# First ada sums on TensorE, norms scaled on DVE, attention normed early and first in the output product, a square root in the convolution: the mixer of a fused two-block kernel

## The chip, the cores and the metric

One Trainium2 chip, one core of it. The metric is the device time of one execution in microseconds (us). Engines are named as in the profile: PE is TensorE's matrix multiplication, PEld its weight load, DVE VectorE, ACT ScalarE, POOL GpSimd, SP SyncE, whose queue issues nearly all DMAs. Before the change the median of 3 runs is 2957.59 us (2957.12 to 2958.0).

## The reference, cut to what matters

512 tokens of width 1024 run through a first block (a mixer of attention and a gated convolution, then a layer of 16384 experts) and a second one (two more layers with attention, a recurrence and feed-forward parts). The change touches the first block's mixer and the start of the expert layer:

```python
ada = silu(c) @ w_ada + b_ada                       # six vectors of 1024
shift1, scale1, gate1, shift2, scale2, gate2 = split(ada, 6)
h = rms_norm(x, norm1_g) * (1 + scale1) + shift1
proj = h @ w_in + b_in                              # q, k, v, then three gates of the convolution
attn = head_rms_norm(sliding_window_sink_attention(q, k, v, sinks), attn_out_g, 8)
conv = head_rms_norm(b_gate * conv3(c_gate * u), conv_out_g, 8)
x = x + gate1 * (concatenate([attn, conv]) @ w_out + b_out)
h2 = rms_norm(x, norm2_g) * (1 + scale2) + shift2
q = h2 @ w_query                                    # scores against two key tables, top 16 of each
x = x + gate2 * experts(h2, top 16 of the sums)
```

All is in float32. A product is made of three matmuls in a reduced format: each operand is split into a high and a low part, and high x high, low x high and high x low are summed.

## The kernel before, in words

The kernel is one Python class that writes out every instruction; a framework puts each engine's instructions in an order at compile time, sets the semaphores, and gives out buffers of a named ring (a tag with a number of buffers) as the instructions that first write them are placed. A block under `issue_after(ins)` puts what it traces on that instruction's engine behind it.

`mixer0` begins with the ada vectors. `ada1(k)` (L396) loads, for two columns of 128, four pieces of w_ada of 512 KB through the ring `raw` (4 buffers, shared with all weight loads), and `ada_acc` (L333) sums them on DVE, one row block of 128 at a time, eight for each vector; a matmul with ones (`ptc`, L359) then adds over the partitions. The four token tiles of x are normed by `rms_tokens` (L314): square with a sum on ACT, root on ACT, reciprocal on DVE, scaling on ACT for this first norm (L328) and on DVE for all others (L326). `to_fm` (L275) transposes the normed tokens on PE, applies scale and shift on ACT and DVE, and splits them. Four such column pairs run one after the other, with the first five weight chunks of w_in between.

The product with w_in has 18 chunks of 128 output columns; `consume(n, ps)` (L432) takes each. Chunks 0 to 4 are q and k, 5 is v, after which `sw_block` (L507) writes out the attention of four blocks of 128 tokens with two head groups each. Chunks 6 to 17 are four convolution groups of three chunks each; with the third chunk of a group (n = 8, 11, 14, 17) the group is convolved on DVE, squared on ACT, summed over 64 channels by a matmul with a block matrix (`ptms`, L478), put through Ln and Exp on ACT (L479, L480) and split into `mixh` and `mixl`. Beside it, four pieces per chunk of the remaining ada vectors (gate1, scale2, shift2) are loaded into the ring `mix` (8 buffers, shared with the mixh and mixl tiles) and summed on DVE; their closing matmuls (`ends`) run two chunks after. The PSUM ring `pst` (2 buffers, tag t) serves ptc, the attention's scores and transposes, ptms and the transposes of `to_fm`.

After the 18 chunks `sw_finish` (L559) norms the attention's output over heads and transposes it (`pto`, L572) into split tiles in the rings xh and xl. The output product (`gemm_tm`) runs in two halves of 512 columns, four token tiles of eight row blocks each; the order of the row blocks is three convolution groups, four attention tiles, the last convolution group, and w_out's rows are laid out to match. In the first half all four token tiles advance together, one row block at a time. `consume2` (L495) adds gate1 times the result to x. Then the second norm and `to_fm` give the input of the expert layer, `xs2`, with a copy of 128 tokens kept (`keep`, L309). `peer_route` multiplies by w_query in 16 chunks, and DVE finds the top 16 of each score row with MAX8 and its companions (`top16`, L593).

`to_fm` has a parameter `late`: with it, all columns of the first three token tiles are done first, and all columns of the last token tile after them. The ring `b4` (4 buffers of 1024 floats) holds normed tokens and the attention's scores S.

Of the kernel before, what the change touches and what calls it, by code (L numbers as in the profile page):

```python
# [10 lines left out]
F32 = mybir.dt.float32  # L11
# [56 lines left out]
def _layout(i):  # L68
# [25 lines left out]
    L["w_out"] = _kh(np.concatenate([i["w_out"][512:896], i["w_out"][:512], i["w_out"][896:]]), 2)  # L94
# [63 lines left out]
class _Kernel:  # L158
# [155 lines left out]
    def rms_tokens(self, x, pool, d=1024, fast=True):  # L314

        nc = self.nc
        xn = []
        for t in range(4):
            j = self.work.tile([128, d], F32, tag="sq", name="sq", bufs=1)
            ss = self.small.tile([128, 1], F32, tag="ss", name="ss", bufs=4)  # L320
            nc.scalar.activation(j, x[t], AF.Square, accum_out=ss)
            r = self.small.tile([128, 1], F32, tag="r", name="r", bufs=4)
            self.rstd(r, ss, 1.0 / d, self.eps6)
            o = pool.tile([128, d], F32, tag="b4", name="xn", bufs=4) if pool else x[t]
            if fast:
                nc.vector.tensor_scalar(o, x[t], r, None, ALU.mult)  # L326
            else:
                nc.scalar.activation(o, x[t], AF.Copy, scale=r)  # L328
            xn.append(o)
        return xn  # L330
# [34 lines left out]

    def ada_row(self, s, brow, out, pool, later=None):
        nc = self.nc
        nc.sync.dma_start(out, bass.AP(tensor=self.a["rows"].tensor,
                                       offset=self.a["rows"][_ROWS.index(brow)].offset,
                                       ap=[[0, 128], [1, 1024]]))  # L370
        for c0 in range(0, 1024, 512):
            yield from self.ada_acc(s, c0, 512, pool, None)

            def end(acc=self.acc, c=slice(c0, c0 + 512)):
                pt = (self.pst or self.psa).tile([128, 512], F32, tag="t" if self.pst else "a", name="ptr")
                nc.tensor.matmul(pt, self.ones, acc)
                nc.vector.tensor_tensor(out[:, c], pt, out[:, c], ALU.add)

            later.append(end) if later is not None else end()
            yield  # L380


    def mixer0(self):
# [3 lines left out]
        with tc.tile_pool(name="m0", bufs=1) as p:  # L387
# [11 lines left out]
            first, xt = ada1(0), []  # L399
# [5 lines left out]
            xn = self.rms_tokens(xt, p, fast=False)  # L405
# [22 lines left out]
            mixh, mixl, bo = [], [], []  # L428
            vt = p.tile([128, 4, 128], F32, name="vt")

            def consume(n, ps):
                b = self.col("b_in", n)  # L432
                if n == 12:
                    bo.append(self.brow(p, "b_out", "b4", 4))
# [24 lines left out]
                else:  # L459
                    j, g = divmod(n - 6, 3)  # L460
# [18 lines left out]
                    nc.scalar.activation(r, pt, AF.Ln, bias=self.eps6, scale=1.0 / 64)  # L479
                    nc.scalar.activation(r, r, AF.Exp, scale=-0.5)  # L480
# [7 lines left out]
            mx = list(zip(mixh, mixl))  # L488
            mix = mx[:3] + self.sw_finish(p, oall) + mx[3:]
# [15 lines left out]
            self.xs2 = self.to_fm(self.rms_tokens(x1, p), A2, ada["B2"], keep=self.h2)  # L505
# [52 lines left out]
    def sw_finish(self, p, oall):  # L558
# [3 lines left out]
        for n in range(4):  # L562
            sq = p.tile([128, 1024], F32, tag="b4", name="osq", bufs=4)
            nc.scalar.activation(sq[:, 0:512], oall[:, n, :], AF.Square)
            nc.vector.tensor_reduce(ss[:, n * 8:(n + 1) * 8], sq[:, 0:512].rearrange("p (h d) -> p h d", d=64), AX.X, ALU.add)
# [3 lines left out]
        for j in range(4):  # L569
# [6 lines left out]
            h = self.xpool.tile([128, 512], F32R, tag="xh", name="xh", bufs=8)  # L576
            l = self.xpool.tile([128, 512], F32R, tag="xl", name="xl", bufs=8)
# [25 lines left out]
    def peer_route(self, p, G, fill, step):  # L603
# [52 lines left out]
        self.gemm_fm(self.xs2, [a["w_query"][c] for c in range(16)], consume)  # L656
# [709 lines left out]
```

## Time and profile before

| | |
|---|---|
| median of 3 runs | 2957.59 us (2957.12 to 2958.0) |
| the profiled execution | 2946.67 us, its span 2944.9 us |
| mean granted TensorE clock of it | 0.983 |
| PE busy | 2816.2 us (96%) |
| PEld busy | 2382.1 us (81%) |
| DVE busy | 1963.8 us (67%) |
| ACT busy | 1132.1 us (38%) |
| POOL busy | 332.7 us (11%) |

The span goes from the first to the last instruction; what lies between it and the execution's time is start and end. Busy times are sums of modelled durations, and matmuls overlap: two that follow each other by 0.23 us show 0.39 us each. In the lines of the profile a group reads: line, engine, operation, output<-inputs with the buffer numbers left out, shapes, count, then busy time in us, mean ns of one, idle time of the engine just before and who ended it. In a timeline a line begins with start and duration in us; a bracket at its end gives idle time before it and what released it.

### The profile page before, as it was taken

To read this page: it belongs to the slowest core of one execution; us is meant where nothing else is said; L and a number is where in the kernel's file an instruction comes from. 1 tells how busy PE (TensorE), PEld (TensorE's weight loads), DVE (VectorE), ACT (ScalarE), POOL (GpSimd) and SP (SyncE) were. 2 spreads that over 40 slices of the span, in tenths; PEclk is the share of its full clock that TensorE was granted. 3 is DMA by queue.
4 is the path that set the end of the run, shared out by engine and by line. 5 is a ranking of instruction groups with operands and counts; after the bars stand their busy time and mean duration, and the time that the engine had idled before them with its cause. 6 is when DMAs were issued, how large, how long until landed. Compare 5 with 4: busy or idle time off the path is not lost.

```text
span 2944.9 us, 37577 instructions
## 1 busy us (share of the span) xinstructions
PE 2816.2 (96%) x14133; PEld 2382.1 (81%) x14133; DVE 1963.8 (67%) x3665; ACT 1132.1 (38%) x1672; POOL 332.7 (11%) x265
## 2 busy tenths in 40 slices
PE   6999959889999999999999999999999999999998
PEld 5777858788899999988787778888878887888887
DVE  8676999898778777886557666433474567634336
ACT  4454325566333333333346424222242233422223
POOL 0000023221334433440000000000000000000000
PEclk9999979899999999999999999999999999999999
DMA  8432368778999988899763103232321212323331
GB/s 294 149 105 86 101 199 301 284 295 315 361 320 323 323 313 307 312 325 308 229 188 119 57 29 115 89 118 94 100 91 63 86 58 65 115 86 112 102 95 51
DMA packets 182007, 521.34 MB, mean 177 GB/s; under 512 B 19776, under 2 KB 68544, under 8 KB 180288
## 3 DMA queue, kind: packets, MB, share of 16 engines
q1 hardware_dynamic: 144960, 384.70, 38.7%
q0 software_dynamic: 36864, 134.23, 12.8%
q8 instruction: 111, 1.82, 0.3%
q14 instruction: 72, 0.59, 0.1%
HBM read 478.48 MB, written 40.37 MB: 176 GB/s over the span
## 4 chain that ended last, share of the span: by engine, by line
PE 47%; DVE 2%; DMA 1%; ACT 0%; issue 0%; SPq 0%; DVEq 0%; ACTq 0%
PE psa L205 7%; PE psa L204 7%; PE psa L206 7%; PE psv L204 3%; PE psv L205 3%; PE psv L206 3%; PE psd L206 3%; PE psd L204 3%; PE psd L205 3%; PE pl L1274 1%; PE y L205 1%; PE y L206 1%; PE y L204 1%; PE pss L1013 1%; PE pt L289 1%; PE po L1030 1%
## 5 line engine op out<-in xcount | busy, mean ns | idle before, releaser
L186 ACT ACTIVATE wh<-raw 128x1024 fp32r<-128x1024 f32 x512 | 539.0, 1060 | 1199.3 <-PE psa L205 427.5
L189 DVE TENSOR_TENSOR wl<-raw,wh 128x1024 fp32r<-128x1024 f32 x510 | 620.3, 1222 | 338.4 <-ACT wh L186 323.9
L204 PE MATMUL psa<-xh,wh 128*128 128x512 f32 x1168 | 460.4, 397 | 4.3 <-ACT xh L300 2.8
L205 PE MATMUL psa<-xl,wh 128*128 128x512 f32 x1168 | 460.4, 395 | 1.9 <-DVE xl L307 1.9
L206 PE MATMUL psa<-xh,wl 128*128 128x512 f32 x1168 | 458.0, 393 | 0.5 <-DVE wl L189 0.5
L206 PE MATMUL psu<-xh,wl 128*128 128x384 f32 x1024 | 347.7, 340 | 22.3 <-DVE wl L189 22.3
L204 PE MATMUL psu<-xh,wh 128*128 128x384 f32 x1024 | 349.6, 341 | 16.0 <-ACT ga L798 11.6
L205 PE MATMUL psu<-xl,wh 128*128 128x384 f32 x1024 | 348.2, 340 | 0.0
L205 PE MATMUL y<-wl,wgh 128*128 128x512 f32 x768 | 299.6, 390 | 4.6 <-DVE wl L189 4.6
L206 PE MATMUL y<-wh,wgl 128*128 128x512 f32 x768 | 299.9, 391 | 0.0
L204 PE MATMUL y<-wh,wgh 128*128 128x512 f32 x768 | 298.9, 389 | 0.2 <-ACT wgh L186 0.2
L204 PEld LDWEIGHTS psa<-xh,wh 128*128 128x128 f32 x1168 | 220.8, 190 | 55.2 <-ACT xh L300 6.9
L205 PEld LDWEIGHTS psa<-xl,wh 128*128 128x128 f32 x1168 | 220.4, 189 | 48.1 <-DVE xl L307 3.6
L206 PEld LDWEIGHTS psa<-xh,wl 128*128 128x128 f32 x1168 | 220.4, 189 | 46.1 <-issue 1.0
L206 PEld LDWEIGHTS psu<-xh,wl 128*128 128x128 f32 x1024 | 194.8, 190 | 24.0 <-DVE wl L189 23.9
L204 PEld LDWEIGHTS psu<-xh,wh 128*128 128x128 f32 x1024 | 194.9, 190 | 23.1 <-ACT ga L798 13.9
L754 POOL DMA_INDIRECT row<-in_peer_u_rows,ui x128 | 162.2, 1267 | 426.1 <-DVE junk L761 242.0
L754 POOL DMA_INDIRECT row<-in_peer_v,vi x128 | 164.8, 1288 | 276.0 <-DVE y L770 256.4
L205 PEld LDWEIGHTS psu<-xl,wh 128*128 128x128 f32 x1024 | 194.8, 190 | 1.2 <-issue 0.5
L204 PE MATMUL psv<-wh,xh 128*128 128x512 f32 x464 | 185.4, 400 | 4.2 <-ACT xh L298 2.8
L205 PE MATMUL psv<-wl,xh 128*128 128x512 f32 x464 | 183.9, 396 | 0.0
L770 DVE SCALAR_TENSOR_TENSOR y<-row,au,y 128x1024 f32<-128x1024 f32 x127 | 162.8, 1282 | 30.8 <-DMA row<-in_peer_v,vi 30.2
(331 smaller groups left out, 4379.1 us busy)
## 6 DMA issues: line engine op xcount, KB each, us to landing
raw<-in_peer_u SPq DMA_DIRECT2D x128, 512.0 KB
raw<-in_peer_v SPq DMA_DIRECT2D x128, 512.0 KB
raw<-in_ffn_in SPq DMA_DIRECT2D x88, 512.0 KB
G<-gt SPq DMA_DIRECT2D x12, 2048.0 KB
g<-G SPq DMA_DIRECT2D x192, 128.0 KB
raw<-in_ffn_dn SPq DMA_DIRECT2D x44, 512.0 KB
rawa<-in_w_ada SPq DMA_DIRECT2D x64, 256.0 KB
AD<-ga SPq DMA_DIRECT2D x56, 192.0 KB
```

The source lines that it names most:

```text
L186: nc.scalar.activation(h, full, AF.Copy)
L189: (nc.gpsimd if pool else nc.vector).tensor_tensor(l, full, h.bitcast(F32), ALU.subtract)
L204: nc.tensor.matmul(out, A[0], B[0], start=first, stop=False)
L205: nc.tensor.matmul(out, A[0], B[1], start=False, stop=False)
L206: self.last_mm = nc.tensor.matmul(out, A[1], B[0], start=False, stop=last)
L289: nc.tensor.transpose(pt[:, (t - t0) * 128:(t - t0 + 1) * 128], xn[t][:, k * 128:(k + 1) * 128], self.ident)
L754: nc.gpsimd.indirect_dma_start(out=r, out_offset=None, in_=table, in_offset=bass.IndirectOffsetOnAxis(ap=idx[:, j:j + 1], axis=0))
L770: nc.vector.scalar_tensor_tensor(w, r, au[:, j:j + 1], w, ALU.mult, ALU.add)
L1013: nc.tensor.matmul(ps[:, :W], qr[h // 2][rb:rb + 64, q], kr[rb:rb + 64, :W], start=False, stop=True)
L1030: nc.tensor.matmul(po[:, q], v[j][:, h * 128:(h + 1) * 128], et[:, j * 128:(j + 1) * 128], start=j == 0, stop=j == i)
L1274: nc.tensor.matmul(pt[:P, o:o + 64], k[:, h, c * 128:c * 128 + P], qv[:, c, :, 1])
```

## The change

- The first pair of ada columns is summed by matmuls: `ada_pe` loads the same four pieces in the same order and multiplies each 128x128 block of w_ada by one column of silu(c), accumulating in PSUM over the eight row blocks; the other three pairs stay on DVE.
- All norms scale on DVE; a root of one column is computed at the start (`warm`).
- `sw_finish` is called in `consume` at n = 11, ahead of that chunk's convolution, with its squares in the ring `et` and its split results in `b4`; the attention tiles come first in the output product, then the four convolution groups, and w_out's rows are laid out in that order.
- The row b_out goes into the ring `sq` of the pool `work`.
- The convolution's norm takes a square root on ACT and a reciprocal on DVE (`rstd`) in place of Ln and Exp.
- The second norm's `to_fm` is called with `late=True`; the first four weight chunks of w_query are loaded ahead of the product, the third and fourth with their DVE instructions behind the last scaling of the norm.

```diff
-    L["w_out"] = _kh(np.concatenate([i["w_out"][512:896], i["w_out"][:512], i["w_out"][896:]]), 2)
+    L["w_out"] = _kh(i["w_out"], 2)
...
-            if fast:
-                nc.vector.tensor_scalar(o, x[t], r, None, ALU.mult)
-            else:
-                nc.scalar.activation(o, x[t], AF.Copy, scale=r)
+            self.last_norm = nc.vector.tensor_scalar(o, x[t], r, None, ALU.mult)
...
+    def ada_pe(self, s, bias, out, plus, lo):
+
+        nc = self.nc
+        pt = self.pst.tile([128, 512], F32, tag="t", name="pta")
+        ts = []
+        for k0 in range(0, 8, 4):
+            ts.append(self.wpool.tile([128, 4, 256], F32, tag="raw", name="rawa", bufs=4))
+            nc.sync.dma_start(ts[-1], self.a["w_ada"][s, k0:k0 + 4, :, lo:lo + 256].rearrange("k p n -> p k n"))
+            if k0 == 0:
+                yield
+        for j in range(2):
+            for k in range(8):
+                nc.tensor.matmul(pt[:, j:j + 1], ts[k // 4][:, k % 4, j * 128:(j + 1) * 128], self.sc[:, k:k + 1],
+                                 start=k == 0, stop=k == 7)
+        j0 = lo // 128
+        nc.vector.scalar_tensor_tensor(out[:, j0:j0 + 2], pt[:, 0:2], plus, self.col(bias, j0, 2), ALU.add, ALU.add)
+        yield
...
-            first, xt = ada1(0), []
+            warm = self.small.tile([128, 1], F32, name="warm", bufs=1)
+            nc.scalar.activation(warm, self.eps6, AF.Sqrt)
+            first, xt = itertools.chain(self.ada_pe(1, "b_scale1", ada["s1p"], 1.0, 0),
+                                        self.ada_pe(0, "b_shift1", ada["B1"], 0.0, 0)), []
...
-            xn = self.rms_tokens(xt, p, fast=False)
+            xn = self.rms_tokens(xt, p)
...
-                    bo.append(self.brow(p, "b_out", "b4", 4))
+                    bo.append(self.brow(self.work, "b_out", "sq"))
...
+                    if n == 11:
+                        attn.extend(self.sw_finish(p, oall))
...
-                    nc.scalar.activation(r, pt, AF.Ln, bias=self.eps6, scale=1.0 / 64)
-                    nc.scalar.activation(r, r, AF.Exp, scale=-0.5)
+                    self.rstd(r, pt, 1.0 / 64, self.eps6)
...
-            mx = list(zip(mixh, mixl))
-            mix = mx[:3] + self.sw_finish(p, oall) + mx[3:]
+            mix = attn + list(zip(mixh, mixl))
...
-            self.xs2 = self.to_fm(self.rms_tokens(x1, p), A2, ada["B2"], keep=self.h2)
+            self.xs2 = self.to_fm(self.rms_tokens(x1, p), A2, ada["B2"], keep=self.h2, late=True)
...
-            sq = p.tile([128, 1024], F32, tag="b4", name="osq", bufs=4)
+            sq = p.tile([128, 512], F32, tag="et", name="osq", bufs=2)
...
-            h = self.xpool.tile([128, 512], F32R, tag="xh", name="xh", bufs=8)
-            l = self.xpool.tile([128, 512], F32R, tag="xl", name="xl", bufs=8)
+            hl = p.tile([128, 2, 512], F32R, tag="b4", name="at", bufs=4)
+            h, l = hl[:, 0], hl[:, 1]
...
-        self.gemm_fm(self.xs2, [a["w_query"][c] for c in range(16)], consume)
+        ws = {n: self.wload(a["w_query"][n]) for n in range(2)}
+        with self.tc.issue_after(self.last_norm.ins):
+            ws.update({n: self.wload(a["w_query"][n]) for n in range(2, 4)})
+        self.gemm_fm(self.xs2, [a["w_query"][c] for c in range(16)], consume, ws=ws)
```

## Rows read from the trace of the kernel before

**Rows 1.** Windows: each engine's busy us in a stretch, clock, DMA share, GB/s.

```profile
core 0: us, PE busy (x) PEld busy (x) DVE busy (x) ACT busy (x) POOL busy (x), PEclk, DMA share, GB/s
0.00:20.00 20.00, 3.77 (x16) 3.21 (x16) 10.86 (x39) 15.65 (x24) 0.70 (x6) 1.00 0.91 320
65.00:180.00 115.00, 114.40 (x577) 91.08 (x576) 84.96 (x153) 58.95 (x134) 0.00 (x0) 1.00 0.45 149
180.00:219.00 39.00, 32.95 (x137) 24.65 (x136) 26.08 (x38) 20.60 (x25) 0.00 (x0) 0.87 0.35 110
273.00:440.00 167.00, 134.79 (x674) 117.05 (x673) 165.88 (x977) 53.12 (x71) 24.30 (x21) 0.90 0.42 138
```

**Rows 2.** DVE's groups by line and shape, 0 to 270 us.

```profile
L346 DVE SCALAR_TENSOR_TENSOR acc<-rawa,sc,acc 128x256 f32<-128x256 f32 x56 | 24.3, 479 | 0.4
...
L326 DVE TENSOR_SCALAR xn<-x,r 128x1024 f32<-128x1024 f32 x4 | 3.0, 752 | 0.1
...
L273 DVE RECIPROCAL ss<-ss 128x32 f32<-128x32 f32 x1 | 0.3, 346 | 0.0
...
L1161 DVE RECIPROCAL om<-om 128x8 f32<-128x8 f32 x1 | 0.2, 204 | 0.0
```

**Rows 3.** Timelines of ACT and DVE, 8 to 30 us.

```profile
16.14 1.04 ACT L321 ACTIVATE sq<-x 128x1024 f32<-128x1024 f32 x1
...
18.45 1.13 ACT L328 ACTIVATE xn<-x,r 128x1024 f32<-128x1024 f32 x1
...
17.66 0.15 DVE L273 RECIPROCAL r<-r 128x1 f32<-128x1 f32 x1
18.58 1.23 DVE L189 TENSOR_TENSOR wl<-raw,wh 128x1024 fp32r<-128x1024 f32 x1 [0.77 <-ACT wh L186]
```

**Rows 4.** Timeline of PE, two closings of ada sums, 8 to 60 us.

```profile
10.04 1.02 PE L359 MATMUL ptc<-ones,acc 128*128 128x1 f32 x4 [10.04 <-DVE acc L346]
...
54.99 0.51 PE L359 MATMUL ptc<-ones,acc 128*128 128x1 f32 x4
```

**Rows 5.** Timeline of PE, 160 to 250 us: the output product.

```profile
179.93 0.39 PE L204 MATMUL psv<-wh,mixh 128*128 128x512 f32 x1
...
180.59 1.05 PE L359 MATMUL ptc<-ones,acc 128*128 128x1 f32 x8
...
187.01 0.50 PE L204 MATMUL psv<-wh,mixh 128*128 128x512 f32 x1 [2.07 <-ACT mixh L186]
...
197.32 2.07 PE L478 MATMUL ptms<-cvr,blk 128*128 128x512 f32 x2 [3.95 <-ACT cvr L476]
...
215.67 0.40 PE L206 MATMUL psv<-wh,xl 128*128 128x512 f32 x1
...
240.74 0.39 PE L206 MATMUL psv<-wh,mixl 128*128 128x512 f32 x1
```

**Rows 6.** Timelines of ACT and DVE, 160 to 200 us.

```profile
168.08 0.63 ACT L480 ACTIVATE cvr<-cvr 128x512 f32<-128x512 f32 x1
168.73 1.28 ACT L272 ACT_TABLE_LOAD   x1
...
171.00 2.29 DVE L568 TENSOR_TENSOR oall<-oall,ss 128x2048 f32<-128x2048 f32 x1
...
178.73 0.74 DVE L346 SCALAR_TENSOR_TENSOR acc<-rawa,sc,acc 128x512 f32<-128x512 f32 x1
...
189.93 0.48 DVE L471 TENSOR_SCALAR cvo<-z,cols 128x512 f32<-128x512 f32 x1
```

**Rows 7.** Timelines of DVE and ACT, 230 to 275 us.

```profile
236.33 0.69 DVE L498 TENSOR_TENSOR x<-x,wo 128x512 f32<-128x512 f32 x1
...
245.62 0.75 DVE L326 TENSOR_SCALAR xn<-x,r 128x1024 f32<-128x1024 f32 x1
...
258.68 0.78 ACT L300 ACTIVATE xh<-pt,B,A 128x512 fp32r<-128x512 f32 x1 [0.16 <-PE pt L289]
...
263.68 0.78 ACT L300 ACTIVATE xh<-pt,B,A 128x512 fp32r<-128x512 f32 x1 [0.16 <-PE pt L289]
...
273.31 0.48 DVE L598 MAX8 v<-sc 128x8 f32<-128x128 f32 x2
```

More of the change, by code (lines that the diff above doesn't have):

```diff
@@ L312, in to_fm, with rms_tokens @@
         return [xs[k] for k in ks]
-    def rms_tokens(self, x, pool, d=1024, fast=True):
+    def rms_tokens(self, x, pool, d=1024):
         nc = self.nc
@@ L404, in mixer0 @@
                 xt.append(x)
-            xn = self.rms_tokens(xt, p, fast=False)
+            xn = self.rms_tokens(xt, p)
+            self.first_norm = self.last_norm
             xs, ws = [], {}
@@ L427, in mixer0 @@
             conv_in = {}
-            mixh, mixl, bo = [], [], []
+            mixh, mixl, bo, attn = [], [], [], []
             vt = p.tile([128, 4, 128], F32, name="vt")
@@ L562, in sw_finish @@
         for n in range(4):
-            sq = p.tile([128, 1024], F32, tag="b4", name="osq", bufs=4)
-            nc.scalar.activation(sq[:, 0:512], oall[:, n, :], AF.Square)
-            nc.vector.tensor_reduce(ss[:, n * 8:(n + 1) * 8], sq[:, 0:512].rearrange("p (h d) -> p h d", d=64), AX.X, ALU.add)
+            sq = p.tile([128, 512], F32, tag="et", name="osq", bufs=2)
+            nc.scalar.activation(sq, oall[:, n, :], AF.Square)
+            nc.vector.tensor_reduce(ss[:, n * 8:(n + 1) * 8], sq.rearrange("p (h d) -> p h d", d=64), AX.X, ALU.add)
         self.rstd(ss, ss, 1.0 / 64, self.eps6)
```

## The prediction, made before the changed kernel was run

> **What bounds the kernel now.** Only the first 245 of 2945 us are touched, so I read the stages first (windows), then who waits in them (the timeline of each engine), then single rows for prices. The windows [rows 1] show three kinds of stage. From 65 to 180 us PE is busy 114.4 of 115: whatever arrives earlier in front moves everything behind it by as much. From 180 to 219, about the first half of the output product, PE is busy 32.95 of 39 at a mean granted clock of 0.87: time is lost there. From 273 to 440, the routing, DVE is busy 165.88 of 167: the rest of the program starts when DVE gets its first scores, so the row to watch is the first MAX8 at 273.31 [rows 7], not the first matmul of w_query. I make the sum up to this MAX8 and carry it to the end unchanged.
>
> **Front: first ada sums and norms.** Now the first column pair takes two chains of eight steps on DVE, up to 0.479 us each (L346 [rows 2]), 7.4 us in all with a shorter first step, and ScalarE scales four tiles at 1.13 us [rows 3]. The last scaled tile ends at 19.58, and DVE begins the first weight split at 18.58 [rows 3]; from there DVE works nearly without a gap on the next pair's splits, bias steps and sums.
> After: the scalings cost DVE 4 x 0.752 (L326 [rows 2]). The last tile of x lands near 13.6, an estimate: 4.1 MB at the 320 GB/s of the first 20 us [rows 1] take 12.8 us, plus the start. From the start of a square to the end of its reciprocal the trace has 16.14 to 17.81 [rows 3], 1.67 us; with the scaling the tile is ready at 16.0, and DVE starts the splits some 2.4 us earlier. TensorE's price: each `ada_pe` is 16 matmuls of 128x128 by one column. Two such are four records, 1.02 us early and 0.51 us later [rows 4], so 16 cost 4.1 to 8.2 us, both together 8.2 to 16.3. PE has nothing else to do before 16 us, and the weights land at 5 to 12.5 us. At the slow price throughout, B ends at 21.5, some 4 us later than now, and two of the four `raw` buffers are held as long; with the quick price from the middle on it ends near 17. Value: 1.5 us earlier. Bounds: 4 earlier (all that ACT and DVE are relieved of at the end of the chain), 4 later. `warm` is one table load while x lands, in ACT's idle time: nothing. SP's queue waits for the same ring as now.
>
> **Middle: attention normed early and first, root in the convolution.** The second half of the product ends at 241.1; from 215.67 to 240.74 there are 108 steps of 0.232 us, so its 96 matmuls take 22.3 and the first half ran from 179.93 to about 218.8, 38.9 us [rows 5]. It needs 22.3 plus about 5.0 of small matmuls (an estimate: two ptc at 0.9 by spacing after their row's 1.05, three ptms and four pto at about half of what their rows show). So 11.6 us are waits and slow clock, among them 2.07 for the second convolution tile and 3.95 for the third [rows 5].
> With attention in front the convolution tiles are needed 11 to 20 us later. What is late next? Buffers of `pst` go out in program order: the code's order ptc, ptms, ptms, pto is the trace's, with ptc at 180.59 and pto last, after 197.32 [rows 5]. In the new code pto stands behind the ptc of 180.59, which waits for sums of which one runs at 178.73 [rows 6]. oall is scaled at 173.3 [rows 6], but its transposes can't start before 180.6. Then transposes 0.4, scaling 0.75, rounding 0.63 (as the Exp's 512 wide row [rows 6]): first product matmul at 182.6, a wait of 2.4 us behind w_in's last matmul.
> Then DVE. From 180.6 to the last convolution tile it has six sums of 0.74 (4.5), four attention tiles of 0.75 + 0.69 (5.7, as a 512-wide sum [rows 6] and a 512-wide addition [rows 7]), the last convolution's 3.4, three times 0.75 + 0.68 (4.3) and three reciprocals of 128x512. Those are not in the trace. 128x8 takes 0.204 and 128x32 0.346 [rows 2], 5.9 ns an element more, so 128x512 would take 3.2 us. Bounds: 0.48 (the cheapest 128x512 on DVE [rows 6]) and 5.5 (0.346 / 32 for each element); I take 3.2, from the slope at the larger row. That is 27.5 us if DVE never idles and all of it lies ahead. By the ring alone (the last `cvo` waits for the second one's release, as at 189.93 [rows 6]) I get 25.5. Value: 26. PE comes to that tile after 2.0 + 7 x 2.78 + 2 = 23.5 us, so 2.5 us of wait are left. Gain: 11.6 - 2.4 - 2.5 = 6.7. Bounds: 11.6 (no wait at all), and a loss of 1.7 (reciprocals of 5.5: 6.9 more on DVE, 34.4 in all, 10.9 of wait).
> On ACT the edit removes per group an Exp of 0.63 and two table loads of 1.28 [rows 6]. On the path of a group 0.69 + 3.2 stand in place of 0.69 + 1.28 + 0.63, 1.3 us longer: the root is no gain by itself, it fits only because the tiles are needed later.
> A page speaks against it too. The Trainium skill, "VectorE: DVE Perf Modes", section "First, the fixed hardware budget", says that Reciprocal is an iterative divide with a repeat count of 8. Read as eight steps per element at the 0.96 GHz that the Trainium skill's "Trainium Kernel Development and Optimization" gives in "NeuronCore Architecture", an estimate is 4.3 us each, 3.3 more over three, and a middle gain of 3.4. The slope of the rows is lower, and the sum goes by them.
> At no cost: the squares in `et` (free after the attention blocks), b_out's row in `sq` (its DMA and five DVE instructions move into 65 to 180, where DVE is busy 84.96 of 115 [rows 1]), w_out's row order. Attention now holds the four `b4` buffers until the last quarter of the product, so two tiles of the second norm wait for that; the third one is later anyway. Without this cover it would cost up to 4 us.
>
> **Behind the product: late=True and early w_query weights.** The product ends at E = 241.1 [rows 5], MAX8 is at E + 32.2. Today the last normed tile is at 246.4, and each of eight columns takes 2.5 us (two in 258.68 to 263.68 [rows 7]), with w_query's matmuls between. After: three tokens' tiles go first. The third tile of x is complete at 237.0 [rows 7]; with no weight split ahead of it the norm (1.67 + 0.75) gives E - 1.7, in place of about E + 3.3. Eight columns of 384 take 2.5 - 0.33 = 2.17 us each (an estimate: a quarter off two passes of 0.8 less their fixed part, and one transpose), 17.3 in all. w_query's matmuls read whole 512-wide tiles, so none runs until the last token's part comes, about 1.5 later. Then two chunks, 48 x 0.232 = 11.1, about 2 for the slow clock that PE's pause brings, 3 for the scores: E + 33 to 35. Value: 1.5 us lost. Bounds: 4 gained (the third chunk no longer runs ahead of the second's end), 12.4 lost (below).
>
> **Sum.** -1.5 - 6.7 + 1.5 = -6.7. The profiled execution took 2946.67 (span 2944.9) and becomes 2940.0. The median of the runs lies 10.9 above it; the difference carries over: 2957.6 - 6.7 = 2950.9.
>
> **Rivals.**
> Late transposes decide. If the third tile comes no earlier than now (+4.9), and three chunks run interleaved as now, so that the second ends with the third (+5.5), and the clock is slow (+2), MAX8 moves to E + 44.6: 12.4 lost, and with -1.5 and -6.7 the whole is +4.2, 2961.8. It decides from 8.2 us of loss. For it: the 384-wide phase leaves PE without matmuls for 17 us. Against: all eight columns are complete some 5 us earlier than now, and DVE needs only two chunks.
> DVE becomes the bound of the first half: the reciprocals take their upper bound, the middle loses 1.7, the whole is +1.7, 2959.3. For: DVE is busy 26.08 of 39 there [rows 1], 13 free, hardly more than four reciprocals. Against: rows give a slope that falls with size.
> Both waits of the middle vanish: were `pst` not given in program order, pto would run at 173.3 and the product would find all its tiles: -1.5 - 11.6 + 1.5 = -11.6, 2946.0, with a front of -4 2943.5. For: only one ring's rows speak for the order, and DVE has more time then.
>
> **How the numbers follow.** Forecast (a gain of 3 to 11 us, 2946.5 to 2954.5) 0.50; late transposes 0.13; DVE the bound 0.20; both waits gone 0.17. No change is what lies within 0.2%, 5.9 us, about what a measurement of this kernel can tell. The forecast is beyond that in 0.36 of its 0.50, the last rival in all of its 0.17; DVE's case is no change in 0.16 and slower in 0.04; late transposes split 0.06 and 0.07. So faster 0.53, same 0.36, slower 0.11. The range 2939 to 2962 takes in the bounds of front and middle on one side and the first rival on the other.
>
> **What would show it.** Front: the first weight split on DVE near 16, w_in's first matmul near 18; wrong if the second pta ends after 20. Middle: pto directly behind a ptc near 179, the product's first matmul, with attention's tiles, some 2 us later, a RECIPROCAL of 128x512 near 3.2 us, a short wait ahead of the last convolution tile, the first half under 34 us; wrong if PE waits over 6 us there. Behind: no w_query matmul until about 17 us after the product, MAX8 33 to 35 after it. Beyond MAX8 no stage should differ by more than a few us; if one does, the sum fails whatever the front does.

## The result and the profile after

The changed kernel takes 2977.55 us (median of 6 runs, 2973.42 to 2984.68) where the kernel before took 2956.6 beside it: a ratio of 1.0078, 95% interval 1.0062 to 1.0094. It is slower by 21 us; 2950.9 was predicted, in a range up to 2962. The profiled execution took 2973.42 (span 2971.7), 26.75 above that of before; it lies 4.1 under its median, that of before 9.9 under its own, which is the difference to 21.

Eight rows of each trace divide the 26.75: the first `B` (DVE's bias step of the first column pair), the fourth `B`, the copy of `vt` (start of attention), the first and the last matmul of the output product, the first w_query matmul, the first MAX8 (to which the prediction made its sum) and the first gather on POOL, which stands behind all of the routing. E is the start of the product's last matmul here; the prediction's E is its end, 0.4 us later. Starts in us, each from the timeline of its engine:

| kernel | first B | 4th B | vt | product from | E | w_query | MAX8 | gather |
|---|---|---|---|---|---|---|---|---|
| before | 17.58 | 56.90 | 75.26 | 179.93 | 240.74 | 247.77 | 273.31 | 391.41 |
| after | 21.11 | 66.48 | 89.25 | 197.35 | 257.13 | 277.85 | 292.89 | 416.51 |

Front (to vt): +14.0, predicted -1.5. Middle (vt to E): 165.48 becomes 167.88, +2.4, predicted -6.7. Behind the product (E to MAX8): 32.57 becomes 35.76, +3.2, predicted +1.5. Routing (MAX8 to the gather): 118.10 becomes 123.62, +5.5, which the prediction carried over as unchanged. Together 25.1; the other 1.7 fall after the gather. All were wrong on the same side.

PE in the front of the changed kernel (timeline: start, us busy, engine, line, operation, out<-in, count, in brackets the idle time ahead and its releaser):

```profile
5.55 1.84 PE L375 MATMUL pta<-sc,rawa 128*128 128x1 f32 x8 [5.55 <-DMA rawa<-in_w_ada]
8.24 6.99 PE L375 MATMUL pta<-sc,rawa 128*128 128x1 f32 x32 [0.85 <-DMA rawa<-in_w_ada]
...
15.96 5.12 PE L375 MATMUL pta<-sc,rawa 128*128 128x1 f32 x24
20.94 1.93 PE L289 MATMUL pt<-ident,xn 128*128 128x128 f32 x6
23.53 0.79 PE L204 MATMUL psa<-xh,wh 128*128 128x512 f32 x1 [0.66 <-ACT xh L300]
...
29.10 0.63 PE L205 MATMUL psa<-xl,wh 128*128 128x512 f32 x1
29.53 0.63 PE L206 MATMUL psa<-xh,wl 128*128 128x512 f32 x1
```

64 records take 13.95 us, 0.218 each. That is near the slow price of [rows 4] (0.255) from first to last, and never the quick one (0.128). The 512-wide matmuls behind them come every 0.43 us until 29.53; [rows 5] have 0.232 for such a matmul. The first w_in matmul is at 23.53 where PE's timeline of the kernel before has it at 21.25.

DVE around the fourth `B`, first in the changed kernel, then in the kernel before (timeline, same columns):

```profile
61.91 0.16 DVE L357 SCALAR_TENSOR_TENSOR s1p<-ptc,cols 128x2 f32<-128x2 f32 x1 [2.58 <-PE ptc L356]
...
62.40 0.15 DVE L431 TENSOR_TENSOR A<-s1p,cols 128x2 f32<-128x2 f32 x1
62.47 3.92 DVE L343 SCALAR_TENSOR_TENSOR acc<-rawa,sc,acc 128x512 f32<-128x512 f32 x7
66.48 0.16 DVE L357 SCALAR_TENSOR_TENSOR B<-ptc,cols 128x2 f32<-128x2 f32 x1
```

```profile
55.53 0.16 DVE L360 SCALAR_TENSOR_TENSOR s1p<-ptc,cols 128x2 f32<-128x2 f32 x1 [0.83 <-PE ptc L359]
...
56.00 0.15 DVE L411 TENSOR_TENSOR A<-s1p,cols 128x2 f32<-128x2 f32 x1
56.07 0.75 DVE L346 SCALAR_TENSOR_TENSOR acc<-rawa,sc,acc 128x512 f32<-128x512 f32 x1
56.90 0.16 DVE L360 SCALAR_TENSOR_TENSOR B<-ptc,cols 128x2 f32<-128x2 f32 x1
```

A row of the timeline that merges several instructions shows the shape of the first alone. The seven sums of the changed kernel are of two shapes (lines by form, 62.50 to 66.45):

```profile
L343 DVE SCALAR_TENSOR_TENSOR acc<-rawa,sc,acc 128x512 f32<-128x512 f32 x4 | 3.0, 747 | 0.0
L343 DVE SCALAR_TENSOR_TENSOR acc<-rawa,sc,acc 128x256 f32<-128x256 f32 x3 | 1.4, 480 | 0.0
```

The engines execute in the order written when the kernel is built, and that order is another one now. The three 256-wide sums belong to this column pair; the four 512-wide ones are sums of the later ada vectors, and one of these stood there before. Counted from the start, six 512-wide sums stand ahead of this `B`, where three stood. SyncE's queue is in another order too (timeline of the changed kernel): w_in's sixth chunk, which `vt` needs, is asked for behind 16 loads of w_ada, where it was 12, at 65.74 in place of 51.76.

```profile
43.50 0.34 SPq L195 DMA_DIRECT2D raw<-in_w_in  x1
43.89 21.79 SPq L337 DMA_DIRECT2D rawa<-in_w_ada  x16
65.74 0.42 SPq L195 DMA_DIRECT2D raw<-in_w_in  x1
```

The first half of the product in the changed kernel, which answers to [rows 5, 6]: DVE with the last two of its three reciprocals of that stretch, then PE (timelines).

```profile
214.51 3.35 DVE L273 RECIPROCAL cvr<-cvr 128x512 f32<-128x512 f32 x1 [0.55 <-ACT cvr L272]
217.78 0.65 DVE L494 SCALAR_TENSOR_TENSOR cvo<-z,cols,cvo 128x512 f32<-128x512 f32 x1
...
221.42 0.69 DVE L496 TENSOR_TENSOR cvo<-cvo,cv 128x512 f32<-128x512 f32 x1
...
224.71 3.35 DVE L273 RECIPROCAL cvr<-cvr 128x512 f32<-128x512 f32 x1 [0.33 <-ACT cvr L272]
```

```profile
195.21 1.07 PE L592 MATMUL pto<-ident,oall 128*128 128x128 f32 x8
...
217.09 0.40 PE L206 MATMUL psv<-wh,mixl 128*128 128x512 f32 x1
219.82 0.50 PE L204 MATMUL psv<-wh,mixh 128*128 128x512 f32 x1 [2.33 <-ACT mixh L186]
...
222.82 1.12 PE L500 MATMUL ptms<-cvr,blk 128*128 128x512 f32 x2
229.56 0.79 PE L204 MATMUL psv<-wh,mixh 128*128 128x512 f32 x1 [5.62 <-ACT mixh L186]
230.16 0.63 PE L205 MATMUL psv<-wl,mixh 128*128 128x512 f32 x1
```

The last group's own convolution step (217.78) stands behind the reciprocal of the group before it, so its sum of squares is late, so its own reciprocal is, and PE stops for 2.33 and 5.62 us. DVE is hardly ever free in this stretch. Two windows, from the first scaling of an attention tile to the end of the last scaling of `cvo`, and behind PE's second stop (window, us, busy time and count of PE, PEld, DVE, ACT, POOL, granted clock, DMA share, GB/s), then a line by form of the first of them:

```profile
195.88:228.85 32.97, 25.32 (x110) 18.49 (x108) 31.68 (x34) 10.08 (x14) 0.00 (x0) 0.99 0.29 91
229.56:234.85 5.29, 5.29 (x12) 4.08 (x13) 3.95 (x6) 0.00 (x0) 0.00 (x0) 0.50 0.00 0
```

```profile
L189 DVE TENSOR_TENSOR wl<-raw,wh 128x1024 fp32r<-128x1024 f32 x5 | 6.0, 1220 | 0.0
```

After the second stop a matmul comes every 0.43 us until 234.8, at a granted clock of 0.50, where [rows 5] have 0.232: the two levels of the clock, 1.2 and 2.4 GHz.

Behind the product, PE in two of the 384-wide columns of the changed kernel (timeline), then the window around them:

```profile
264.10 0.48 PE L310 MATMUL ptk<-ident,full 128*128 128x128 f32 x1 [1.48 <-DVE full L306]
264.37 0.85 PE L289 MATMUL pt<-ident,xn 128*128 128x128 f32 x3
266.54 0.47 PE L310 MATMUL ptk<-ident,full 128*128 128x128 f32 x1 [1.33 <-ACT full L300]
...
269.14 0.48 PE L310 MATMUL ptk<-ident,full 128*128 128x128 f32 x1 [1.48 <-DVE full L306]
```

```profile
260.00:280.00 20.00, 10.09 (x37) 6.51 (x38) 11.19 (x18) 10.58 (x25) 0.00 (x0) 0.56 0.31 101
```

A column takes 2.5 us, as the 512-wide ones of [rows 7] did, and the first w_query matmul is at 277.85, E + 20.7.

The scores of w_query's first two chunks, ACT's copies `sc` (timelines), first in the changed kernel, then in the kernel before, and what DVE waited for between MAX8 and the gather of the changed kernel (waits: us in total, times, longest):

```profile
292.26 0.60 ACT L655 ACTIVATE sc<-ptsc 128x512 f32<-128x512 f32 x1 [1.41 <-issue]
...
296.62 0.60 ACT L655 ACTIVATE sc<-ptsc 128x512 f32<-128x512 f32 x1 [1.25 <-PE ptsc L651]
```

```profile
272.03 0.59 ACT L635 ACTIVATE sc<-ptsc 128x512 f32<-128x512 f32 x1
272.85 0.60 ACT L635 ACTIVATE sc<-ptsc 128x512 f32<-128x512 f32 x1 [0.22 <-PE ptsc L631]
```

```profile
DVE v L618 <- ACT sc L655: 3.7, 5, 1.3
```

The kernel before has no such wait there. Its second chunk's scores are at E + 32.1, those of the changed kernel at E + 39.5.

### The profile page after: what moved, and what is told of

Same layout as the page of the kernel before. It is cut to its first block, busy times and chain, and to the rows that moved or that the text cites. A ratio compares the mean times of both kernels' runs of the same rounds, so it can differ in the third digit from the quotient of the medians.

```text
span 2971.7 us, 37695 instructions
## 1 busy us (share of the span) xinstructions
PE 2839.5 (96%) x14189; PEld 2398.4 (81%) x14189; DVE 1977.8 (67%) x3669; ACT 1118.0 (38%) x1669; POOL 333.9 (11%) x265
## 4 chain that ended last, share of the span: by engine, by line
PE 47%; DVE 2%; DMA 1%; ACT 0%; issue 0%; SPq 0%; DVEq 0%; ACTq 0%
PE psa L204 7%; PE psa L205 7%; PE psa L206 7%; PE psv L204 3%; PE psv L206 3%; PE psv L205 3%; PE psd L206 3%; PE psd L204 3%; PE psd L205 3%; PE pl L1298 1%; PE y L205 1%; PE y L206 1%; PE y L204 1%; PE pss L1037 1%; PE pt L289 1%; PE po L1054 1%
## 5 line engine op out<-in xcount | busy, mean ns | idle before, releaser
L204 PE MATMUL psv<-wh,xh 128*128 128x512 f32 x432 | 172.8, 400 | 4.2 <-ACT xh L298 2.8
L205 PEld LDWEIGHTS y<-wl,wgh 128*128 128x128 f32 x768 | 144.1, 188 | 39.6 <-DVE wl L189 10.1
```

What stands on the lines that cost most here:

```text
L204: nc.tensor.matmul(out, A[0], B[0], start=first, stop=False)
L205: nc.tensor.matmul(out, A[0], B[1], start=False, stop=False)
```

## The experiments

Times are medians, each with a ratio to the kernel before run beside it (median 2955.3 to 2956.7). Table of the same starts for all kernels:

| kernel | first B | 4th B | vt | product from | E | w_query | MAX8 | gather | us | ratio, 95% interval |
|---|---|---|---|---|---|---|---|---|---|---|
| e1 | 18.80 | 57.81 | 76.73 | 185.34 | 245.09 | 266.10 | 280.86 | 404.48 | 2964.2 | 1.0013 to 1.0041 |
| e2 | 21.05 | 65.29 | 87.78 | 195.85 | 255.98 | 261.73 | 288.31 | 407.56 | 2971.1 | 1.0036 to 1.0070 |
| e3 | 20.66 | 64.84 | 87.29 | 195.42 | 246.20 | 267.56 | 281.39 | 404.81 | 2970.3 | 1.0034 to 1.0067 |
| e4 | 18.12 | 56.84 | 76.40 | 184.24 | 236.20 | 241.80 | 268.88 | 388.16 | 2949.2 | 0.9973 to 0.9995 |
| e5 | 24.04 | 63.67 | 81.82 | 187.54 | 248.34 | 255.37 | 280.68 | 398.83 | 2958.1 | 0.9996 to 1.0020 |
| e6 | 17.52 | 57.76 | 76.30 | 181.21 | 248.85 | 255.88 | 282.01 | 400.17 | 2960.4 | 1.0007 to 1.0032 |
| e7 | 18.60 | 59.06 | 76.97 | 182.92 | 245.06 | 269.33 | 283.89 | 407.46 | 2971.6 | 1.0025 to 1.0058 |
| e8 | 21.46 | 64.84 | 87.53 | 195.55 | 255.66 | 276.82 | 291.11 | 414.77 | 2977.2 | 1.0053 to 1.0092 |
| e14 | 21.45 | 65.69 | 85.50 | 191.90 | 253.24 | 273.94 | 289.11 | 412.75 | 2975.0 | 1.0038 to 1.0073 |
| e16 | 22.73 | 63.53 | 81.70 | 193.20 | 251.61 | 272.77 | 287.24 | 410.86 | 2973.4 | 1.0050 to 1.0093 |
| e17 | 21.39 | 62.98 | 83.08 | 191.34 | 251.00 | 272.04 | 286.78 | 410.42 | 2970.4 | 1.0032 to 1.0064 |
| e10 | 17.83 | 57.72 | 75.94 | 186.24 | 241.44 | 247.18 | 273.86 | 393.12 | 2954.5 | 0.9982 to 1.0005 |
| e11 | 18.10 | 58.18 | 76.09 | 185.59 | 241.59 | 247.19 | 274.38 | 393.66 | 2955.5 | 0.9987 to 1.0008 |
| e13 | 18.02 | 58.57 | 76.76 | 186.69 | 241.88 | 248.88 | 274.30 | 392.45 | 2955.6 | 0.9983 to 1.0005 |
| e18 | 17.85 | 56.60 | 76.03 | 183.27 | 238.86 | 244.45 | 271.61 | 390.87 | 2951.5 | 0.9979 to 1.0012 |
| e19 | 18.19 | 57.07 | 76.14 | 181.09 | 241.93 | 248.95 | 274.26 | 392.31 | 2954.2 | 0.9981 to 1.0009 |

Each row of starts is one profiled execution. Where the written order in front is that of before (e6, e7), vt varies from 75.26 to 76.97; and behind the gather, where no edit reaches, the traces take from 2550.1 us (e2) to 2570.1 (e5). So a us or two of a start, and a whole profiled time, decide nothing by themselves.

**One part undone at a time, and three together (e1 to e4).**

e1, the first ada sums back on DVE:
```
-first, xt = itertools.chain(self.ada_pe(1, ...), self.ada_pe(0, ...)), []
+first, xt = ada1(0), []
```


> The changed kernel, with the first ada sums back on VectorE in place of TensorE; everything else as changed. Theory (one-column matmuls at about 0.22 us a record hold TensorE and the raw buffers, and the whole chain of w_in loads shifts): the vt copy comes back from 89.25 to 74-77 us, B of the first pair to about 17 from 21.1, the whole to 2961-2965 (13 to 15 us less than the changed kernel). Rival (the scaling of the norm on VectorE or the order of SyncE's loads does it): vt stays above 85 and the whole above 2972.

e2:
```
-self.xs2 = self.to_fm(..., keep=self.h2, late=True)
+self.xs2 = self.to_fm(..., keep=self.h2)
```


> The changed kernel with late=True taken away (the second norm's transposes as in the kernel before); the early w_query weights stay. Theory (the late order delays the columns and leaves TensorE slow): from the last product matmul to the second chunk's scores 4 to 7 us come back, the whole is 2970-2974. Rival (the early w_query weights cost it): less than 2 us change, above 2975.

e3:
```
-self.rstd(r, pt, 1.0 / 64, self.eps6)
+nc.scalar.activation(r, pt, AF.Ln, bias=self.eps6, scale=1.0 / 64)
+nc.scalar.activation(r, r, AF.Exp, scale=-0.5)
```


> The changed kernel with Ln and Exp on ScalarE back in the three convolution groups in place of the square root with a reciprocal on VectorE. Theory (the 3.35 us reciprocals in VectorE's in-order queue delay the convolution tiles, TensorE waits 2.3 and 5.6 us for them): the product's first half shortens by 6 to 9 us, the whole is 2968-2972. Rival (attention ahead of the convolution in the ring of PSUM buffers is what costs): the first half stays within 2 us, the whole above 2975.

e4 makes the three edits together.


> The changed kernel without the TensorE sums, without the square root in the convolution and without late=True: what is left of the change is attention normed early and first in the product, the first norm scaled on VectorE and the early w_query weights. Theory (three separate losses hide a gain of the attention order): 2945-2952, 5 to 12 us under the kernel before, with the gain between the end of attention and the last product matmul (77 us before, under 71 here). Rival (the attention order gains nothing): 2955-2960, as before.

All four medians came out as the theories had them, and so did the stages, nearly: e1 has its first `B` at 18.80 where about 17 was expected, and in e2 the second chunk's scores come 7.6 us earlier behind E where 4 to 7 were. Against 2977.55 the three give back 13.3, 6.5 and 7.2 us, 27.0 in all, and e4 28.4: three separate losses that add up. Each shows in its own stage: e1 has vt at 76.73; e2 has 151.6 us from E to the gather against 159.4 (3.4 of the difference up to MAX8, 4.4 behind it); e3 has 50.8 from the first product matmul to E against 59.8. PE's only waits in that stretch of e3 (timeline) are short:

```profile
214.84 1.12 PE L500 MATMUL ptms<-cvr,blk 128*128 128x512 f32 x2 [1.54 <-ACT cvr L498]
221.59 0.50 PE L206 MATMUL psv<-wh,mixl 128*128 128x512 f32 x1 [0.61 <-DVE mixl L189]
```

And in e2 the window that stood at a clock of 0.56 has PE at work (windows, columns as above):

```profile
260.00:280.00 20.00, 18.34 (x72) 13.06 (x73) 10.64 (x14) 9.11 (x16) 0.00 (x0) 0.74 0.24 79
```

e4 beats both kernels, by 0.05 to 0.27% against the kernel before. From the last matmul of attention to E it takes 70.6 us where the kernel before takes 77.3, as its theory had it.

**One part alone in the kernel before (e5 to e7).** The edits are those of e1 to e3 the other way round.

> The kernel before with one edit of the change, the first ada sums on TensorE; the order of SyncE's loads stays exactly as before. Theory (the sums on TensorE are the whole front loss): B of the first pair at 20-22 us from 17.6, the vt copy at 86-90 from 75.3, the whole 2968-2972. Rival (the loss needs the norm on VectorE beside it, or the other order of the loads): vt under 80, the whole within 4 us of the kernel before.

> The kernel before with one edit of the change, the square root with a reciprocal on VectorE in the three convolution groups. Theory (three 3.35 us reciprocals in VectorE's in-order queue delay the convolution's tiles, which are multiplied first here): the first half of the product grows by 4 to 10 us, the whole is 2961-2967. Rival (a reciprocal costs only where attention's tiles share VectorE with it; by itself it replaces Ln, Exp and two table loads at about the same price): within 2 us of the kernel before.

> The kernel before with one edit of the change, late=True in the second norm's transposes. Theory (the 384-wide columns cost 2.5 us each as the 512-wide ones do, the 128-wide ones come on top, TensorE falls to its lower clock): 4 to 8 us slower, 2961-2965, with no w_query matmul until 17 us or more after the product. Rival (late costs only with the early w_query weights or the product's later end): within 2 us of the kernel before.

e6: the product grows from 60.8 to 67.6 us, PE's waits of [rows 5] become these (timeline), and the time rises by 4.3 us, a little under what the theory had:

```profile
191.89 0.80 PE L204 MATMUL psv<-wh,mixh 128*128 128x512 f32 x1 [5.97 <-ACT mixh L186]
204.34 0.80 PE L204 MATMUL psv<-wh,mixh 128*128 128x512 f32 x1 [3.40 <-ACT mixh L186]
```

So the root costs in either order of the product. e7: late alone costs more than expected, 11.7 us from E to the gather (6.3 up to MAX8, 5.5 behind it) and 7 to 17 us by the ratio. e5 fell between the theories: with the orders of DVE's column pairs and SyncE's loads as before, vt is 6.6 late in its profile, nothing grows behind the first `B` (39.6 us from first to fourth, 39.3 before, 45.4 after), and the median moves by 2.0, interval -1.2 to 5.9. That the sums on TensorE alone make the 14 us is wrong.

**What makes 3.5 us into 14 (e8, e14, e16, e17).**

e8, other buffers for the weights of the sums:
```
-ts.append(self.wpool.tile([128, 4, 256], F32, tag="raw", name="rawa", bufs=4))
+ts.append(pool.tile([128, 2, 256], F32, tag="mix", name="rawp", bufs=8))
```


> The changed kernel, with the weights of the TensorE sums in buffers of their own (eight of 128x2x256 in the mix ring, which is idle then) in place of the four raw buffers. Theory A (holding the raw buffers until the slow sums end is what delays all later weight loads): B of the first pair stays at about 21, but the vt copy comes back from 89.25 to 77-82 and the whole to 2964-2970. Theory B (the late B itself, and TensorE's time, set the front): vt stays above 86, the whole above 2974.

e14:
```
-for n in range(len(ws), min(5, len(ws) + 2)):
+for n in range(len(ws), min(6, len(ws) + 2)):
```


> The changed kernel with w_in's sixth chunk asked for together with the first five (min(6, ...) in place of min(5, ...)), so that in SyncE's queue it no longer stands behind the sixteen w_ada loads of 43.9 to 65.7 us. The TensorE sums stay. Theory C (the growth of the front's loss from 3.5 us at the first B to 14 at vt comes from the queue orders: the sixth chunk's load behind those loads, its split on VectorE at 79.45 in place of 64.78): first B unchanged at about 21, vt at 78-83, the whole 2966-2972. Theory B (the late first B and TensorE's time alone): vt stays above 86, the whole above 2974.

e16, the norm's scaling on ScalarE as before:
```
-xn = self.rms_tokens(xt, p)
+xn = self.rms_tokens(xt, p, fast=False)
```


> The changed kernel with the first norm's scaling back on ScalarE; the TensorE sums stay. The order written for VectorE and SyncE in front is then that of the kernel before. Theory D (the growth of the loss in front comes from the written order that goes with both edits together): first B still at 21-24, but the fourth B not more than 7 us after the 56.9 of before and vt at 80-83, the whole 2963-2970. Rival (the TensorE sums alone make the growth): vt above 86, the whole above 2973.

e17, an order given to DVE alone (`b4` is the bias step of the fourth pair):
```
-for _ in range(4):
-    next(later, None)
+with self.tc.issue_after(b4):
+    for _ in range(4):
+        next(later, None)
```


> The changed kernel with the later ada sums of gate1, scale2 and shift2 queued on VectorE behind the bias step of the fourth column pair (B of the fourth pair), by an order alone; nothing is left out. Theory D (seven 512-wide sums ahead of the fourth B in VectorE's in-order queue, and w_in's sixth chunk behind the sixteen loads that feed them, make the growth): fourth B at 60-63 from 66.5, vt at 80-84 from 89.25, the whole 2966-2972. Rival (the front's growth lies in waits for loads, or the held-back sums are missed later, where gate1 and the second norm need them): vt above 86 or the whole above 2975.

Held buffers (theory A, my first one) fell: in e8 the 14.1 us that SyncE waited for `pta` in the first 35 us of the changed kernel are gone, and 1.7 us come back at vt and 0.3 in the median. The sixth chunk's load (e14) is worth 3.7 us at vt and 2.6 in the median, less than its theory. e17 puts all six 512-wide sums behind the fourth `B`, and has this `B` 3.5, vt 6.2, the gather 6.1 and the median 7.1 us earlier. Its edit orders DVE alone, but SyncE's order follows: the sixth chunk is asked for behind 11 loads, at 56.16 in place of 65.74. So the 3.5 at the fourth `B` are DVE's order; the 2.7 that come on top by vt go with the earlier load, which e14 moved by itself. Its DVE (timeline), to be read beside the two fences of that stretch above:

```profile
60.62 0.16 DVE L357 SCALAR_TENSOR_TENSOR s1p<-ptc,cols 128x2 f32<-128x2 f32 x1 [1.06 <-PE ptc L356]
...
62.98 0.16 DVE L357 SCALAR_TENSOR_TENSOR B<-ptc,cols 128x2 f32<-128x2 f32 x1 [0.76 <-PE ptc L356]
63.05 0.48 DVE L341 TENSOR_SCALAR acc<-rawa,sc 128x512 f32<-128x512 f32 x1
...
83.08 0.68 DVE L478 COPY vt<-ptv 128x512 f32<-128x512 f32 x1
```

e16, whose written order in front is again that of the kernel before, has the same: 81.70 at vt, though its median (runs from 2966.9 to 2983.9) stayed 3 us above what was expected. So of the 14 us some 6 are the written order, and 6 to 8 are the sums' own delay (vt in e5, e16 and e17). DVE's order grew worse only with the TensorE sums and the norm on DVE together: e19 has the norm alone and e5 the sums alone, both with three 512-wide sums ahead of the fourth `B`. The 16 loads ahead of the sixth chunk come with the norm alone, and cost nothing there: e19 asks for it at 59.09 and has vt at 76.14.

**Where the gain of e4 is (e10, e11, e13, e18, e19).** e10 is e4 with e16's edit; e11 and e18 are e10 and e4 with attention's transposes ahead of the later sums' ends; e13 is e10 without the early w_query weights; e19 is the kernel before with the norm on DVE.
```
 due.append(len(ends))
+if n == 11:
+    attn.extend(self.sw_finish(p, oall))
 with self.tc.issue_after(self.last_mm.ins):
...
-if n == 11:
-    attn.extend(self.sw_finish(p, oall))
...
-self.gemm_fm(self.xs2, [a["w_query"][c] for c in range(16)], consume, ws=ws)
+self.gemm_fm(self.xs2, [a["w_query"][c] for c in range(16)], consume)
```


> The version with attention early and first and the early w_query weights (2949.2 us), with the first norm's scaling back on ScalarE. Theory (on VectorE, four scalings stand in the way of the first pair's sums; first B 18.12 against 17.58, vt 76.40 against 75.26): vt near 75, the whole 2945-2948. Rival (the first norm's place is worth nothing): within 2 us of 2949.

> As the version with attention early and first and the norm on ScalarE, but with attention's norm and transposes issued ahead of the later ada sums' ends in the last chunk of w_in, so that pto no longer stands behind a ptc in the ring of PSUM buffers. Theory (pto waits for that ptc's sums, 2 to 3 us): the product's first matmul follows w_in's last one without the wait, 2 to 3 us sooner after the end of attention, the whole 2942-2946. Rival (the wait moves to the sums behind, or VectorE is what attention's tiles wait for): within 1.5 us of the version without it.

> The version with attention early and first and the norm on ScalarE, without the early w_query weights. Theory (loading four chunks of w_query early shortens the way from the product's end to the first scores by 1 to 2 us: 5.6 us to the first w_query matmul against 7.0 before): MAX8 1 to 2 us later, the whole 1 to 2 us longer. Rival (the wait is for the transposed columns, not the weights): no difference beyond 1 us.

> The 2949.2 us version (attention early and first, norm on VectorE, early w_query weights, no TensorE sums, no root in the convolution, no late order), with attention's norm and transposes issued ahead of the later ada sums' ends. Theory (pto's wait behind a ptc costs 1 to 2 us): 2946-2949. Rival (as with the norm on ScalarE, where it changed nothing): within 2 us of 2949-2951.

> The kernel before with one edit of the change, the first norm's scaling on VectorE. Theory (the 7 us gain of the 2949 us version is attention's place, and the norm on VectorE is worth at most 1 to 2 us either way): 2954-2959. Rival (the norm's place alone makes the gain, through another written order): 2948-2951.

e11 and e13 were their rivals' (no difference beyond 1.1 us), e18 is not told apart from e4 or from the kernel before, e19 was its theory's. e10 was nobody's: 5.3 us longer than e4. Its vt is no later, but the windows of the product's start differ, e4 first, then e10 (windows, columns as above):

```profile
180.00:200.00 20.00, 20.00 (x97) 15.94 (x97) 16.79 (x26) 14.55 (x18) 0.00 (x0) 1.00 0.32 97
200.00:220.00 20.00, 16.57 (x69) 12.44 (x68) 12.91 (x19) 7.54 (x9) 0.00 (x0) 1.00 0.30 81
```

```profile
180.00:200.00 20.00, 18.36 (x87) 14.39 (x86) 18.05 (x28) 11.57 (x15) 0.00 (x0) 0.91 0.30 94
200.00:220.00 20.00, 16.00 (x60) 11.92 (x59) 11.36 (x17) 9.86 (x12) 0.00 (x0) 0.91 0.39 130
```

From its first matmul to E the product is shorter in both (52.0 in e4, 55.2 in e10, 60.8 in e19), but it begins later after vt (107.8, 110.3 and 105.0), and in e10 that and the lower clock eat all of it: vt to E is 159.8, 165.5 and 165.8. e11 and e13 have 165.5 and 165.1 there, so this is no accident of one trace; e18 has 162.8. That the other written order does it was not tested. So attention first is worth about 6 us up to E, and only under one of two written orders; in the whole e4 gains 1.5 to 8.0 us on the kernel before.

The early w_query weights gain nothing: MAX8 comes 32.4 us behind E with them (e10) and without (e13). From MAX8 to the gather e2, e4, e10, e11 and e18, which have them, take 119.3 us, and before, e5, e6, e13 and e19, which don't, 118.1 to 118.2.

## Why the prediction was wrong

**Front, -1.5: failed.** The step was the price of the sums. Both ends were worked out, with "B ends at 21.5" for the slow price; I took the quick one from the middle on, though the only early row [rows 4] is slow. PE was still at the lower of its two clock levels then (last section), and the sums cost the slow price to the end: `B` came at 21.11, DVE's first weight split at 22.05 ("near 16") and w_in's first matmul at 23.53 ("near 18"). The test that the prediction set itself ("wrong if the second pta ends after 20") says so. The second error is larger in kind: I took what follows the first `B` to move as a block. It was 3.5 us late at the first `B`, 9.6 at the fourth and 14.0 at vt. The written order moved too, 6 us of the 14 (e17), and no row of before could show that.

**Middle, -6.7: the gain is real, the root eats it.** pto directly behind a ptc, the first product matmul 2.1 us behind that pto (195.21 to 197.35), and the reciprocal's price came as said (and e11 shows that pto's place is worth nothing). Without the root the middle gains 6.6 us: e3 takes 158.9 from vt to E. The step that failed is the sum of DVE's work ahead of the last convolution tile, "Value: 26", and with it the sentence "it fits only because the tiles are needed later". From the start of that ptc (194.32) to the end of the last scaling of `cvo` (228.85) DVE took 34.5 us, and in the last 33.0 of them it was busy 31.7. The three reciprocals are 10.1 of that, 9.6 in the sum. Five weight splits (`wl`), 6.0 us, are not in the sum at all, though the kernel before has five there too (between 180 and 215.5).

With DVE full, each group's steps stand behind the reciprocal of the group before: PE waits 2.33 and 5.62 us where the sum had one wait of 2.5, begins the product 3.5 us behind w_in's last matmul where it had 2.4, and runs 12 matmuls at the lower clock, 2.4 us more (12 times 0.43 less 0.232). The first half takes 37.5 us, where "under 34" was to show. The set mark of 6 us was passed by the sum of the waits, 7.95. The rival "DVE becomes the bound" is what happened, with a wrong reason: the price was 3.35, not 5.5, and the splits made up the rest; that its loss of 1.7 is near the measured 2.4 is luck. Whether another order of the same work on DVE would save part of it was not run.

The Trainium skill, "VectorE: DVE Perf Modes", section "First, the fixed hardware budget", with its repeat count of 8, gave an estimate of 4.3 us for that reciprocal. The trace has 3.35, near the 3.2 by the slope of [rows 2], so read as eight full steps for an element that count is too dear here; the measurement decides.

The Trainium skill, "PSUM — Partial Sum Buffer", section "Engine vs sequencer instructions", says that VectorE's queue is strict first in, first out. The traces agree: DVE stood idle for 0.55 us ahead of the reciprocal of 214.51, and the step of 217.78, which reads nothing of it, still came right behind it.

**Behind the product, +1.5: nearly right up to MAX8, and failed behind it.** From the end of the last product matmul MAX8 came after 35.4 us, where "33 to 35" was to show: 3.2 lost for 1.5. The 2.17 us for a column of 384 took a quarter off the passes. A column is a chain over PE and the copies instead: three transposes, the copy to `full`, the transpose back (`ptk`) that waits 1.3 to 1.5 us for it, and behind that, in PE's queue, the next column's transposes. The width hardly enters: 2.5 us, as at 512. The 128-wide columns then take 1.4 each (277.34 to 288.7 for eight).

The step that failed is another: "I make the sum up to this MAX8 and carry it to the end unchanged." The first MAX8 needs the first chunk's scores alone, and the routing needs the others in time. Before, the first two chunks ran interleaved with the transposes and their scores came 0.8 us apart; now they are 4.4 apart, and DVE, which never waited for scores before, does so five times, 3.7 us of the 5.5. Every kernel with late=True takes 123.4 to 123.7 from MAX8 to the gather, with or without the other edits, and every kernel without it 118.1 to 119.3. The rival "late transposes decide" had MAX8 at E + 44.6, which did not come; its price of 12.4 is near what late costs alone by the gather, 11.7 (e7), by another way. Here the two stages lose 8.7.

**Beyond the routing** nothing differs by more than 1.7 us in the profile, as said.

What stays open: why e5's median moves by 2 us where its own profile shows vt 6.6 late (that profile is of the slowest of its 12 runs, 2970.7, and the part behind the gather is 16.6 us longer in it than in that of before), and why the same edits let the order of e4 keep its gain and that of e10 not.

## What to carry to other kernels

Where a planner writes the queues' order, an edit that changes two early steps can reorder everything behind them: before pricing the block behind an edit as moved, compare the written orders of the two kernels. Before filling an engine's free time, list everything that stands in its queue in that stretch: the work that the sum left out (the weight splits) was what the reciprocals collided with. A sum that ends at the first of many items, as at the first MAX8, says nothing of when the later ones come. And if the only row at that point of the kernel is the slow one, the slow price is the value, not the bound.

## What the hardware showed that was not expected

One-column f32 matmuls cost 0.218 us a record for 64 in a row between 5.5 and 21.1 us; 0.128 is what [rows 4] show at 54.99, amid other matmuls. PE had done nothing before 5.55, and the 512-wide matmuls behind the sums come every 0.43 us until 29.53, which is the spacing of the stretch at a granted clock of 0.50 above: PE was at the lower of its two levels. The clock column prints 1.00 for that time all the same, but the trace's first clock record begins only at 30.4 us, so this 1.00 is no reading. Ahead of the first record the spacing of like matmuls tells the level, not the column.

A reciprocal on DVE goes by the element count. Two groups of DVE in the changed kernel between 170 and 230 us (lines by form: busy us, mean ns of one, idle us before them):

```profile
L273 DVE RECIPROCAL cvr<-cvr 128x512 f32<-128x512 f32 x4 | 13.4, 3351 | 1.3 <-ACT cvr L272 1.3
...
L273 DVE RECIPROCAL ss<-ss 128x32 f32<-128x32 f32 x1 | 0.4, 353 | 0.0
```

That is 6.2 ns for each further element of a row, (3351 - 353) / 480, while the 512-wide scalings beside it (L595, L502) take 0.75 us in all.
